# A two-layer diffusion block with expert-choice experts: the experts' residual in tiles of its own, later gathers, and weight rows loaded in pairs

## The chip, the cores and the metric

One core of one Trainium2 chip runs the whole program. The metric is the device time of the slowest (here the only) core in microseconds, as the median of several runs. TensorE does the matrix products, VectorE (DVE), ScalarE (ACT) and GpSimd (POOL) the elementwise work, and SyncE (SP) issues nearly all loads, in one queue, in the order of the program.

## The reference, cut to what matters

Two layers run over 256 latent tokens and 256 context tokens of width 1024 (the second layer finishes the latent tokens alone). Each layer is a token mixer with four branches, a layer norm, and an expert-choice feed-forward:

```python
def expert_choice_ffn(h, w_router, w_gate, w_up, w_down):
    aff = softmax(h @ w_router)                          # per token, over 16 experts
    gval, idx = top_k(swapaxes(aff, 1, 2), 32)           # each expert picks its 32 tokens
    xg = h[idx]                                          # gather
    y = (silu(xg @ w_gate) * (xg @ w_up)) @ w_down       # three 1024x1024 float32 matrices per expert
    y = y * gval[..., None]
    return zeros(n, 1024).at[idx].add(y)                 # scatter

x_lat = layer_norm(alpha * x_lat + g1 * y_lat, ln1_g, ln1_b)
f_lat = expert_choice_ffn(x_lat * (1 + sc2) + sh2, ...)
x_lat = layer_norm(alpha * x_lat + g2 * f_lat, ln2_g, ln2_b)
```

The context tokens go through the same code in the first layer with their own 32 picks per expert. All expert weights are read once in each layer: 16 experts x 3 matrices x 4 MiB = 192 MiB, so 384 MiB for both layers.

## The kernel before, in words

The change lies in `moe(l)` and in what feeds it. After `out_project` the normed tokens stand in `self.xz`, four tiles (layer 0) or two (layer 1) of 128 tokens x 1024. `route` transposes each with TensorE (eight 128x128 blocks) and multiplies them with the router's weights; then VectorE works out softmax and top-k, and `onehot` makes selection matrices from the positions.

**Gather.** `gather(g)` serves experts 4g to 4g+3. For each of the eight 128-wide blocks of the features, and for latent and context tokens apart, two matmuls with a block of `xz` as the stationary and the one-hot matrix as the moving operand bring the picked tokens, transposed, into `xgT`; ACT and DVE apply the layer norm's gain and shift (`c2`) on the way out of PSUM. The one-hot matmuls are in float32, and the trace counts two instructions for each. Gather 0 is interleaved with expert 0. Gathers 1 and 2 stand behind the gate and up matmuls of experts 1 and 2, and gather 3 behind the down matmuls of expert 2. There are four `xg` buffers.

**Residual.** Right behind gather 3, `residual()` broadcasts alpha times the norm's gain and shift over the partitions (32 matmul instructions, tile `ps_gb`) and overwrites `xz` with the residual term on VectorE. It must stand behind the last gather, since a gather reads the `xz` that it overwrites. After each fourth expert the experts' outputs are scattered into `xz` (`ps_f`), and after the last one into `ps_fin`, from which `ln_last` makes the layer's output.

**Weights.** `wl` loads one slot of 1 MiB: 256 rows of a weight matrix as two 128-row blocks, so each partition gets row p and row 128+p, 4 KB each. An expert needs twelve slots. The slots go round in the order of a list, `order2`: in layer 0 seven full slots (one tile of 8 KB per partition, one DMA) and six made of two 4 KB tiles (two DMAs); in layer 1 eleven full and seven split ones. A slot is loaded again when TensorE is done with its last content. Expert 0 has slots of its own besides (`early`), some in buffers of `xg`, so the loads of the first sixteen or so slots run before the experts begin. SP issues the loads in the program's order, so a load that waits for its slot holds up all behind it.

**The modulation weights.** `mod` loads 1 MiB pieces of `w_mod` with 8 KB runs through the same queue and the same tiles (line 234).

Of the kernel before, what the change touches and what calls it, by code (L numbers as in the profile page):

```python
# [15 lines left out]
P = 128  # L16
# [75 lines left out]
class Net:  # L92
# [1038 lines left out]
    def merge(self, l, br, first):  # L1131
# [3 lines left out]
        oT = self.mg.tile([P, 2, 512], F32, tag="oT", name="oTm", bufs=1)  # L1135
        nc.sync.dma_start(oT[:, :, :n], self.oT[br])
        ol = self.mg.tile([P, 2, 512], F32R, tag="ol", name="ol", bufs=1)
        oh = self.mg.tile([P, 2, 512], F32R, tag="oh", name="oh", bufs=1)
# [59 lines left out]

    def xt(self, t):

        return self.xz[:, t - self.xt0]
# [25 lines left out]
    def ln_last(self, l, t, src, rows):  # L1227

        nc = self.nc
        z = self.xt(t)  # L1230
# [13 lines left out]
    def comb(self, name, g, b, sc, sh):  # L1244

        nc = self.nc
        cg = self.keep.tile([P, 8], F32, name=name + "g")
        cb = self.keep.tile([P, 8], F32, name=name + "b")
# [3 lines left out]
        return cg, cb  # L1252


    def router_weights(self, l):
# [4 lines left out]
        nc.scalar.dma_start(wr, self.a["w_router"][l].rearrange("(k p) e -> p k e", p=P))  # L1260
# [15 lines left out]
    def route(self, t, stats):  # L1276
# [20 lines left out]
    def moe(self, l):  # L1297
# [10 lines left out]
        with ExitStack() as mo:  # L1308
# [11 lines left out]
            if nw == 2:  # L1320
                early = {x: [(px, "xg", 4)] for x in (7, 8, 9)}
                early[10] = [(mg, "ol", 1), (pe, "y1", 1)]
            else:
                early = {7: [(px, "xg", 4)] * 2, 8: [(px, "xg", 4), (mg, "ol", 1)]}

            def wl(src, e, kk):

                nonlocal cnt
                rows = src[l, e, kk * 256:(kk + 1) * 256, :].rearrange("(k p) f -> p k f", p=P)
# [5 lines left out]
                if not isinstance(slot, list):  # L1335
                    w = self.wload(rows, (2, 1024), pool=slot)
                    return [w[:, k] for k in range(2)]
                if len(slot) == 1:
                    pool, tag, n = slot[0]
                    w = pool.tile([P, 2, 1024], F32, tag=tag, name="we", bufs=n)  # L1340
                    nc.sync.dma_start(w, rows)
                    return [w[:, k] for k in range(2)]
# [55 lines left out]
            def gather(g):  # L1398

                xgT = px.tile([P, 8, 4, M], F32, tag="xg", name="xgT", bufs=4)  # L1400
# [6 lines left out]
                for kk in range(8 // kn):  # L1407
# [22 lines left out]
            def residual():  # L1430
# [3 lines left out]
                for j in range(2):  # L1434
# [14 lines left out]
            ys = rows = None  # L1449
            for e in range(NE):  # L1450
# [13 lines left out]
                if e in (1, 2):  # L1464
                    self.all_of(gather(e))
# [290 lines left out]
```

## Time and profile before

| | us |
|---|---|
| median of 3 runs | 2164.75 (2156.14 to 2170.97) |
| the profiled execution's own time | 2166.49 |
| its span | 2164.7 |
| layer 0: first gather to the end of the last expert's matmuls | 715.66 to about 1216 |
| layer 1: the same | 1692.15 to about 2155 |

The span is divided into stretches by what the DMA engines do. "DMA share" is the time that packets took on the core's 16 DMA engines, as a share of the stretch; it can go a little above 1, because packets overlap. A stretch at 1.02 or 1.03 is one in which the engines have no gap. MB in the rows is 10^6 bytes; a slot of 1 MiB is 1.049 MB. Busy time of PE is modelled at its ends, so full PE rows say only that work is queued without a gap.

### The profile page before, as it was taken

Reading aid. Unit: us, or ns where it says so; the run is one execution under the profiler, and the core shown is the slowest. Engines: PE = TensorE matmul, PEld = TensorE weight load, DVE = VectorE, ACT = ScalarE, POOL = GpSimd, SP = SyncE. Lnnn points to the kernel's source line nnn. Section 1 sums busy time; section 2 is a strip of 40 time slices with the busy share of each in tenths; the row PEclk is TensorE's granted clock in tenths of the full one; section 3 lists DMA queues with packets and bytes.
Section 4 is the critical chain, followed back from the end, with each engine's and each line's share of the span. In section 5 each row is a group of like instructions: output and inputs, shape, how many; then the busy total and the mean of one; then the engine's idle time right before and its main releaser. Section 6 shows DMA issues by size and latency. Waiting matters only on the chain. (4 is left out here: it accounts for less than half of the span.)

```text
span 2164.7 us, 33549 instructions
## 1 busy us (share of the span) xinstructions
PE 1849.5 (85%) x13730; PEld 1198.9 (55%) x13730; DVE 946.1 (44%) x2139; ACT 503.9 (23%) x1037; POOL 341.2 (16%) x366
## 2 busy tenths in 40 slices
PE   6899899988999899988887898898989886676665
PEld 2677778877879454322222576788889542222221
DVE  3859457854226324121121586967655330010102
ACT  2332217742221110000000332346443110000000
POOL 1151320014431000000000134321274000000000
PEclk9999999999999899999999998989999897776867
DMA  7546412137333599999999465303487899999996
GB/s 291 175 157 209 147 65 88 40 115 251 112 136 112 220 385 347 410 409 409 409 409 409 161 227 183 98 23 106 151 271 268 325 408 409 409 409 409 409 409 255
DMA packets 200182, 553.92 MB, mean 256 GB/s; under 512 B 16223, under 2 KB 83165, under 8 KB 194397
## 3 DMA queue, kind: packets, MB, share of 16 engines
q1 hardware_dynamic: 190960, 538.56, 66.2%
q10 hardware_dynamic: 9068, 13.23, 1.7%
q8 instruction: 108, 1.77, 0.3%
q14 instruction: 46, 0.37, 0.1%
HBM read 541.25 MB, written 10.49 MB: 255 GB/s over the span
## 5 line engine op out<-in xcount | busy, mean ns | idle before, releaser
L1461 PE MATMUL ps_gu<-w,xgT 128*32 128x256 f32 (+1 forms) x1632 | 241.5, 534 | 68.3 <-DMA w<-in_w_up_e_dram 35.0
L149 POOL TENSOR_TENSOR wl<-w,wh 128x1024 fp32r<-128x1024 f32 x62 | 155.2, 2503 | 894.6 <-ACT wh L148 805.4
L1461 PE MATMUL ps_gu<-we,xgT 128*32 128x256 f32 (+1 forms) x1440 | 204.0, 509 | 44.2 <-DMA we<-in_w_up_e_dram 26.3
L1461 PEld LDWEIGHTS ps_gu<-w,xgT 128*32 128x32 f32 (+1 forms) x1632 | 78.3, 134 | 210.5 <-issue 81.1
L1503 DVE TENSOR_TENSOR y<-ps_dn,g2r 32x512 f32<-32x512 f32 (+1 forms) x128 | 70.9, 554 | 254.3 <-PE ps_dn L1492 252.8
L311 PE MATMUL ps_gate<-hh,wh 128*128 128x512 f32 (+1 forms) x512 | 179.4, 351 | 0.4 <-ACT wh L148 0.4
L313 PE MATMUL ps_gate<-hh,wl 128*128 128x512 f32 (+1 forms) x512 | 179.7, 351 | 0.0
L312 PE MATMUL ps_gate<-hl,wh 128*128 128x512 f32 (+1 forms) x512 | 178.2, 348 | 0.0
L148 ACT CAST wh<-w 128x1024 fp32r<-128x1024 f32 x124 | 129.3, 1048 | 178.1 <-PE ps_gate L312 78.2
L1461 PEld LDWEIGHTS ps_gu<-we,xgT 128*32 128x32 f32 (+1 forms) x1440 | 62.0, 127 | 171.9 <-DMA we<-in_w_up_e_dram 63.7
L1492 PE MATMUL ps_dn<-w,eaT 128*32 128x256 f32 (+1 forms) x896 | 119.3, 524 | 28.8 <-DMA w<-in_w_down_e_dram 21.9
L1471 ACT ACTIVATE eth<-ps_gu 128x512 f32<-128x512 f32 (+1 forms) x32 | 15.7, 491 | 515.8 <-PE ps_gu L1461 515.8
L312 PE MATMUL ps_n<-wl,hh 128*128 128x256 f32 x400 | 116.6, 291 | 6.7 <-POOL wl L149 6.7
L1474 DVE SCALAR_TENSOR_TENSOR eac<-eth,ps_gu 128x512 f32<-128x512 f32 (+1 forms) x32 | 17.7, 555 | 238.9 <-PE ps_gu L1461 238.9
L311 PE MATMUL ps_n<-wh,hh 128*128 128x256 f32 x400 | 117.4, 294 | 5.5 <-DVE c_qk L872 3.6
L149 DVE TENSOR_TENSOR wl<-w,wh 128x1024 fp32r<-128x1024 f32 x62 | 85.8, 1384 | 72.4 <-ACT wh L148 72.1
L313 PE MATMUL ps_n<-wh,hl 128*128 128x256 f32 x400 | 116.7, 292 | 0.0
L1492 PE MATMUL ps_dn<-we,eaT 128*32 128x256 f32 (+1 forms) x640 | 91.2, 492 | 17.6 <-DMA we<-in_w_down_e_dram 13.2
L311 PEld LDWEIGHTS ps_gate<-hh,wh 128*128 128x128 f32 x512 | 98.9, 193 | 11.2 <-ACT wh L148 0.8
L313 PEld LDWEIGHTS ps_gate<-hh,wl 128*128 128x128 f32 x512 | 99.1, 193 | 10.8 <-DVE wl L149 0.2
L312 PEld LDWEIGHTS ps_gate<-hl,wh 128*128 128x128 f32 x512 | 98.7, 193 | 10.8
L1473 DVE SCALAR_TENSOR_TENSOR eth<-eth,ps_gu 128x512 f32<-128x512 f32 (+1 forms) x32 | 17.8, 555 | 193.6 <-ACT eth L1471 193.6
(452 smaller groups left out, 3579.4 us busy)
## 6 DMA issues: line engine op xcount, KB each, us to landing
w<-in_w_gate_e_dram SPq DMA_DIRECT2D x75, 1024.0 KB, 13.2
w<-in_w_down_e_dram SPq DMA_DIRECT2D x72, 1024.0 KB, 12.7
w<-in_w_up_e_dram SPq DMA_DIRECT2D x62, 1024.0 KB, 13.3
we<-in_w_up_e_dram SPq DMA_DIRECT2D x120, 512.0 KB, 13.6
w<-in_w_in_dram SPq DMA_DIRECT2D x54, 1024.0 KB, 5.6
we<-in_w_down_e_dram SPq DMA_DIRECT2D x108, 512.0 KB, 14.0
we<-in_w_gate_e_dram SPq DMA_DIRECT2D x96, 512.0 KB, 13.6
w<-in_w_mod_dram SPq DMA_DIRECT2D x44, 1024.0 KB, 5.1
```

Source lines behind the costliest of these rows:

```text
L148: nc.scalar.copy(h, w)
L149: (nc.gpsimd if j else nc.vector).tensor_tensor(x, w, h.bitcast(F32), op=OP.subtract)
L311: nc.tensor.matmul(ps, lh[k], rh[k], start=(k == 0), stop=False)
L312: nc.tensor.matmul(ps, lh[k], rl[k], start=False, stop=False)
L313: nc.tensor.matmul(ps, ll[k], rh[k], start=False, stop=(k == nk - 1))
L1461: nc.tensor.matmul(ps[M * q:M * q + M, :NF], xg[e // 4][:, 2 * kk + k, e % 4, :], w[k][:, q * NF:(q + 1) * NF], start=(kk == 0 and k == 0) ...
L1471: nc.scalar.activation(th, pss[0][:, :NF], AF.Tanh, scale=0.5)
L1473: nc.vector.scalar_tensor_tensor(th, th, 1.0, pss[0][:, :NF], op0=OP.add, op1=OP.mult)
L1474: nc.vector.scalar_tensor_tensor(ac, th, 0.5, pss[1][:, :NF], op0=OP.mult, op1=OP.mult)
L1492: nc.tensor.matmul(py[M * q:M * q + M, :NF], av[:, fc % nj, fc // nj, :], w[k][:, q * NF:(q + 1) * NF], start=(fc == 0), stop=(fc == 7))
L1503: nc.vector.tensor_tensor(ys[w][32 * e4:32 * e4 + 32, q * NF:(q + 1) * NF], py[o:o + 32, :NF], g2r[o:o + 32, q * NF:(q + 1) * NF], op=OP.mult)
```

## The change

1. The residual gets tiles of its own, `acc` (8 KB per partition for two token tiles: two of them in layer 0, one in layer 1). `residual()` reads `xz` and writes `acc`; the scatters, `fin_tiles` and, in layer 1, `ln_last` use `acc`. So `xz` stays whole, and the residual no longer needs all gathers ahead of it: it moves behind the down matmuls of expert 1.
2. Gathers 1, 2 and 3 move to behind the gate and up matmuls of experts 2, 6 and 10. Two `xg` buffers are left of four. The space is `acc`'s, and the early slots that lay in `xg` lie in `xg` and `acc`.
3. Layer 1's final norm rows are made at expert 11 in place of expert 9, in tiles of `xz`.
4. `wl` assigns rows in pairs: partition p gets rows 2p and 2p+1 of the 256, which lie side by side in HBM. A full slot is loaded as one run of 8 KB per partition; a split slot as two DMAs of 4 KB runs, each taking every other row.
5. So that the products still match, all that has the features on the partitions follows the pairs: the gather's stationary blocks, the router's transposes and the transposes of the activations take every other column (`pairs`, a step of two elements), the router's weights are loaded in that order, and `in_pairs` reorders the gains and shifts `c2` with small matmuls against every other column of the identity (16 in layer 0 and 8 in layer 1, each with a stationary block of 128x64 and four moving columns) and two VectorE copies.
6. Some small tiles share buffers across the layers (`comb`, `s2`), and `merge` takes its tile `oh` before `ol`.

```diff
+    def pairs(x):
+        return x.rearrange("p (a q j) -> p a j q", q=P, j=2)
...
+    def in_pairs(self, name, cols):
+        nc = self.nc
+        n = len(cols)
+        ps = self.pt.tile([P, 512], F32, tag="t", name="ps_pair")
+        pv = ps[:, :8 * n].rearrange("p (j i a) -> p j i a", j=2, i=n)
+        for i, c in enumerate(cols):
+            cv = c.rearrange("p (a h) -> p h a", h=2)
+            for h in range(2):
+                for j in range(2):
+                    nc.tensor.matmul(pv[64 * h:64 * h + 64, j, i], self.c("ident").rearrange("p (m j) -> p j m", j=2)[:, j],
+                                     cv[:, h], start=True, stop=True)
+        out = self.keep.tile([P, 4, 8], F32, tag="c2p", name=name, bufs=1)[:, :n]
+        for j in range(2):
+            nc.vector.tensor_copy(out.rearrange("p i (a j) -> p i a j", j=2)[:, :, :, j], pv[:, j])
+        return out
...
-        nc.scalar.dma_start(wr, self.a["w_router"][l].rearrange("(k p) e -> p k e", p=P))
+        nc.scalar.dma_start(wr.rearrange("p (a j) e -> p a j e", j=2),
+                            self.a["w_router"][l].rearrange("(a q j) e -> q a j e", q=P, j=2))
...
-                nc.tensor.transpose(ps[j][:, k * P:(k + 1) * P], z[:, kc * P:(kc + 1) * P], self.c("ident"))
+                nc.tensor.transpose(ps[j][:, k * P:(k + 1) * P], self.pairs(z)[:, kc // 2, kc % 2], self.c("ident"))
...
-                early = {x: [(px, "xg", 4)] for x in (7, 8, 9)}
+                early = {7: [(px, "xg", 2)], 8: [(px, "acc", 2)], 9: [(px, "acc", 2)]}
...
-                early = {7: [(px, "xg", 4)] * 2, 8: [(px, "xg", 4), (mg, "ol", 1)]}
+                early = {7: [(px, "acc", 1)], 8: [(px, "xg", 2), (mg, "ol", 1)]}
...
-                rows = src[l, e, kk * 256:(kk + 1) * 256, :].rearrange("(k p) f -> p k f", p=P)
+                rows = src[l, e, kk * 256:(kk + 1) * 256, :].rearrange("(p k) f -> p k f", k=2)
+                flat = src[l, e, kk * 256:(kk + 1) * 256, :].rearrange("(p k) f -> p (k f)", k=2)
...
-                    w = self.wload(rows, (2, 1024), pool=slot)
-                    return [w[:, k] for k in range(2)]
+                    w = self.wload(flat.unsqueeze(1), (1, 2048), pool=slot)
+                    return [w[:, 0, k * 1024:(k + 1) * 1024] for k in range(2)]
...
-                                nc.tensor.matmul(po, self.xz[:, off[w] + i, k * P:(k + 1) * P],
+                                nc.tensor.matmul(po, self.pairs(self.xz[:, off[w] + i])[:, k // 2, k % 2],
...
-                        z = self.xz[:, t, j * 512:(j + 1) * 512]
-                        nc.vector.tensor_tensor(z, z, gb[0], op=OP.mult)
+                        cs = slice(j * 512, (j + 1) * 512)
+                        z = acc[t // 2][:, t % 2, cs]
+                        nc.vector.tensor_tensor(z, self.xz[:, t, cs], gb[0], op=OP.mult)
                         nc.vector.tensor_tensor(z, z, gb[1], op=OP.add)
...
-                if e in (1, 2):
-                    self.all_of(gather(e))
-                if e == 9 and l == 1:
-                    rows = list(self.norm_rows(1, lambda nm: px.tile([P, 1024], F32, tag="xg", name=nm, bufs=4)))
+                if e in (2, 6, 10):
+                    self.all_of(gather(e // 4 + 1))
+                if e == 11 and l == 1:
+                    free = [self.xz[:, t] for t in range(2)]
+                    rows = list(self.norm_rows(1, lambda nm: free.pop(0)))
...
-                    nc.tensor.transpose(ps[:, j * P:(j + 1) * P], ac[:, j * P:(j + 1) * P], self.c("ident"))
+                    nc.tensor.transpose(ps[:, j * P:(j + 1) * P], self.pairs(ac)[:, j // 2, j % 2], self.c("ident"))
...
-                if e == 2:
-                    self.all_of(gather(3))
+                if e == 1:
+                    acc = [px.tile([P, 2, 1024], F32, tag="acc", name="acc", bufs=nw) for _ in ws]
                     residual()
...
-            self.c2 = {w: self.comb(f"c2_{l}{w}", ...) for w in ws}
+            cols = [self.comb(f"c2_{l}{w}", ...) for w in ws]
+            self.c2p = self.in_pairs(f"c2p{l}", [c[i] for i in range(2) for c in cols])
+            self.c2 = {w: (self.c2p[:, i], self.c2p[:, len(ws) + i]) for i, w in enumerate(ws)}
```

## Rows read from the trace of the kernel before

**Rows 1.** The page: mean busy share of the 16 DMA engines, forty slices, in tenths.

```profile
DMA  7546412137333599999999465303487899999996
```

**Rows 2.** Windows: us, busy us (instructions) of PE, PEld, DVE, ACT, POOL, PEclk, DMA share, GB/s.

```profile
754.00:860.00 106.00, 105.97 (x557) 55.64 (x553) 40.59 (x81) 14.96 (x31) 0.00 (x0) 1.00 0.91 356
860.00:1200.00 340.00, 290.20 (x1224) 87.36 (x1224) 62.69 (x104) 15.87 (x28) 0.00 (x0) 1.00 1.03 408
1700.00:2135.00 435.00, 309.14 (x3199) 125.48 (x3198) 60.28 (x140) 21.30 (x52) 0.00 (x0) 0.77 1.03 408
```

**Rows 3.** The same view, single windows of 10 us.

```profile
750.00:760.00 10.00, 10.00 (x50) 5.73 (x48) 2.74 (x4) 0.00 (x0) 0.00 (x0) 1.00 0.41 143
...
820.00:830.00 10.00, 10.00 (x80) 8.59 (x81) 7.55 (x15) 2.08 (x5) 0.00 (x0) 1.00 0.47 192
...
1690.00:1700.00 10.00, 9.36 (x71) 7.06 (x72) 3.58 (x14) 1.96 (x4) 0.00 (x0) 0.78 0.22 70
1700.00:1710.00 10.00, 10.00 (x145) 6.01 (x148) 1.65 (x5) 1.70 (x4) 0.00 (x0) 1.00 1.01 368
```

**Rows 4.** SP's waits in 754 to 832 us: us in total, times, longest.

```profile
SPq L127 <- PE ps_dn L1492: 32.7, 4, 12.5
SPq L1346 <- PE ps_gu L1461: 17.3, 14, 11.8
```

**Rows 5.** TensorE's timeline: start, us, instructions; where experts 1, 2, gather 3, expert 3 begin.

```profile
754.20 3.17 PE L1461 MATMUL ps_gu<-w,xgT 128*64 128x512 f32 x13
...
785.62 4.40 PE L1461 MATMUL ps_gu<-w,xgT 128*64 128x512 f32 x18
...
816.91 2.87 PE L1416 MATMUL ps_xg<-OH,xz 128*128 128x128 f32 x22
...
828.08 1.94 PE L1461 MATMUL ps_gu<-we,xgT 128*64 128x512 f32 x8
```

**Rows 6.** Windows with the gathers' tile ps_xg alone: PE, PEld, DVE, ACT, PEclk, DMA, GB/s.

```profile
768.00:785.70 17.70, 8.93 (x64) 7.77 (x64) 3.19 (x8) 3.65 (x8) 1.00 0.86 337
```

**Rows 7.** Windows with the residual's tile ps_gb alone: PE, PEld, DVE, PEclk, DMA, GB/s.

```profile
819.00:828.30 9.30, 4.23 (x32) 3.89 (x32) 3.08 (x6) 1.00 0.62 249
```

**Rows 8.** DMA packets of 900 to 1100 us, when expert weights alone are loaded.

```profile
DMA packets 21782, 81.85 MB, mean 409 GB/s; under 512 B 1822, under 2 KB 1822, under 8 KB 21774
```

**Rows 9.** SP's timeline from 1308 us, then DMA packets of 1315:1318, 1316:1318 and 227:230.

```profile
1313.07 0.80 SPq L127 DMA_DIRECT2D w<-in_w_mod_dram  x2
...
DMA packets 171, 1.27 MB, mean 423 GB/s; under 512 B 16, under 2 KB 16, under 8 KB 16
...
DMA packets 124, 0.88 MB, mean 442 GB/s; under 512 B 16, under 2 KB 16, under 8 KB 16
...
DMA packets 166, 1.25 MB, mean 415 GB/s; under 512 B 15, under 2 KB 15, under 8 KB 15
```

**Rows 10.** The page's DMA issues: count, KB each, median us to landing; the full slots.

```profile
w<-in_w_gate_e_dram SPq DMA_DIRECT2D x75, 1024.0 KB, 13.2
w<-in_w_down_e_dram SPq DMA_DIRECT2D x72, 1024.0 KB, 12.7
w<-in_w_up_e_dram SPq DMA_DIRECT2D x62, 1024.0 KB, 13.3
```

**Rows 11.** Weight loads of TensorE, ns min/median/max: the route's, the gathers', and a broadcast column's.

```profile
L1287 PEld LDWEIGHTS ps_xT<-const,xz x48: 137/141/228, 686.2 to 1678.1; 128*128 128x128 f32 x48
...
L1416 PEld LDWEIGHTS ps_xg<-OH,xz x384: 186/192/338, 715.7 to 1746.6; 128*128 128x128 f32 x192
...
L1440 PEld LDWEIGHTS ps_gb<-const,lgb x64: 185/190/192, 819.5 to 1751.7; 128*128 128x128 f32 x64
```

**Rows 12.** The chain that ended last, ahead of layer 1's output projection: start, us, what.

```profile
1648.18 1.78 PE ps_rb L164 x16
1649.96 1.92 PE ps_wrb L1268 x16
```

More of the change, by code (lines that the diff above doesn't have):

```diff
@@ L1225, in ln_hat, with ln_last @@
         nc.vector.tensor_scalar(z, z, mu, rs, op0=OP.subtract, op1=OP.mult)
-    def ln_last(self, l, t, src, rows):
+    def ln_last(self, l, t, src, rows, z):
         nc = self.nc
-        z = self.xt(t)
         mu, rs = self.ln_stats(t, src)
@@ L1246, in comb @@
         nc = self.nc
-        cg = self.keep.tile([P, 8], F32, name=name + "g")
-        cb = self.keep.tile([P, 8], F32, name=name + "b")
+        c = self.keep.tile([P, 2, 8], F32, tag=name[:2] + name[-1], name=name, bufs=1)
+        cg, cb = c[:, 0], c[:, 1]
         nc.vector.tensor_tensor(cg, g, sc, op=OP.mult)
@@ L1335, in wl @@
                 if not isinstance(slot, list):
-                    w = self.wload(rows, (2, 1024), pool=slot)
-                    return [w[:, k] for k in range(2)]
+                    w = self.wload(flat.unsqueeze(1), (1, 2048), pool=slot)
+                    return [w[:, 0, k * 1024:(k + 1) * 1024] for k in range(2)]
                 if len(slot) == 1:
                     pool, tag, n = slot[0]
-                    w = pool.tile([P, 2, 1024], F32, tag=tag, name="we", bufs=n)
-                    nc.sync.dma_start(w, rows)
-                    return [w[:, k] for k in range(2)]
+                    w = pool.tile([P, 2048], F32, tag=tag, name="we", bufs=n)
+                    nc.sync.dma_start(w, flat)
+                    return [w[:, k * 1024:(k + 1) * 1024] for k in range(2)]
                 out = []
@@ L1448, in moe @@
             g0 = next(first)
-            ys = rows = None
+            ys = rows = acc = None
             for e in range(NE):
@@ L1482, in moe @@
                 if e == NE - 1:
-                    fin = {off[0] + i: self.fin_tiles(off[0] + i, pool, tag) for i, (pool, tag) in
+                    fin = {off[0] + i: self.fin_tiles(acc[off[0] // 2][:, i], pool, tag) for i, (pool, tag) in
                            enumerate(((self.pg, "g"), (self.pm, "m")))}
@@ L1521, in moe @@
                     if e == NE - 1 and nw == 2:
-                        fin.update({off[1] + i: self.fin_tiles(off[1] + i, pool, tag) for i, (pool, tag) in
+                        fin.update({off[1] + i: self.fin_tiles(acc[off[1] // 2][:, i], pool, tag) for i, (pool, tag) in
                                     enumerate(((self.pt, "t"), (self.pa, "s")))})
@@ L1531, in moe @@
                                     if hf:
-                                        self.ln_last(l, t + self.xt0, fin[t], rows)
+                                        self.ln_last(l, t + self.xt0, fin[t], rows, self.xz[:, t] if l == 0 else acc[0][:, t])
                                     continue
@@ L1543, in fin_tiles @@
             r.append(pool.tile([P, 512], F32, tag=tag, name="ps_fin"))
-            self.nc.tensor.matmul(r[hf], self.c("ident"), self.xz[:, i, hf * 512:hf * 512 + 512], start=True, stop=False)
+            self.nc.tensor.matmul(r[hf], self.c("ident"), z[:, hf * 512:hf * 512 + 512], start=True, stop=False)
         return r
@@ L1661, in run @@
             v = self.vec[l]
-            s2_ = self.keep.tile([P, 8, 2], F32, name=f"s2{l}")
+            s2_ = self.keep.tile([P, 8, 2], F32, tag="s2", name=f"s2{l}", bufs=1)
             nc.vector.tensor_scalar_add(s2_, self.modc[l][:, 32:40, :], 1.0)
             ws = [0, 1] if l == 0 else [0]
-            self.c2 = {w: self.comb(f"c2_{l}{w}", v[:, R_L1G:R_L1G + 8], v[:, R_L1B:R_L1B + 8], s2_[:, :, w], self.mcol(l, 3, w)) for w in ws}
+            cols = [self.comb(f"c2_{l}{w}", v[:, R_L1G:R_L1G + 8], v[:, R_L1B:R_L1B + 8], s2_[:, :, w], self.mcol(l, 3, w)) for w in ws]
+            self.c2p = self.in_pairs(f"c2p{l}", [c[i] for i in range(2) for c in cols])
+            self.c2 = {w: (self.c2p[:, i], self.c2p[:, len(ws) + i]) for i, w in enumerate(ws)}
             self.g1r = {}
```

9 lines of the change are left out of this document (5 added, 4 removed).

## The prediction

> **What bounds the kernel now.** Read the page's line of DMA shares first [rows 1]: two plateaus of nines, one for each layer's experts. Then the windows [rows 2]: from 860 to 1200 us and from 1700 to 2135 us the DMA share is 1.03 at 408 GB/s, that is, the 16 engines move expert weights without a gap. TensorE is full for 85% of the time in the first plateau (290.2 of 340 us, granted clock 1.00) and for 71% in the second (309.1 of 435 us, granted clock 0.77). In the plateaus the time is bytes over rate, and no engine's work counts. So two things can shorten the experts: a plateau that begins earlier, or a higher rate.
>
> Ahead of layer 0's plateau, 754 to 860 us, it is the other way round: TensorE is busy for 105.97 of 106 us and the DMA moves 356 GB/s in place of 408 [rows 2], with holes of 143 and 192 GB/s [rows 3]. SP's waits say why: it stands up to 12.5 us at a time for slots that `ps_dn` or `ps_gu` still holds [rows 4]. TensorE can't free them, since it does gathers. Layer 1 has no such stretch: its only hole is 1690:1700 us (share 0.22), when expert 0 has just begun, and from 1700 us on the share is 1.01 [rows 3], with gathers 1 to 3 still to come. There TensorE's work is hidden already.
>
> **Gathers and residual: layer 0's plateau begins earlier.** Expert 1 with gather 1 takes 785.62 - 754.20 = 31.4 us of TensorE, expert 2 with gather 2 816.91 - 785.62 = 31.3, gather 3 with the residual 828.08 - 816.91 = 11.2 [rows 5]. One gather is 8.9 us [rows 6], so an expert alone is about 22.4 us, and the residual's matmuls are 4.2 us [rows 7]. The DMA needs 12 x 1.049 MB / 408 GB/s = 30.8 us for an expert. TensorE alone outruns the DMA by 8 us per expert; with a gather in each expert it doesn't.
>
> Now the order after. Expert 0 ends at 754 us as before. Expert 1 without a gather ends at 776.5, the residual at 781, expert 2 with gather 1 at 812, expert 3 at 835 (before: expert 3 began at 828 and so ended about 851). On the DMA side, loads for expert 2 begin as before at 754.5 us, flow from about 756, and are done at 787. Loads for expert 3 need the slots of experts 1's end and expert 2, one after the other: thirteen slots go round, so the first needs expert 1's last slot (776.5), and the k-th later one needs expert 2's k-th, free at 781 + 1.87k. The DMA gets to them at 787 + 2.57k, so it is always later than the slot, also behind the gather (the ninth slot is free at 781 + 8.9 + 16.8 = 806.7, and wanted at 810). The DMA doesn't starve again. All bytes of 754 to 860 us, 106 x 356 = 37.7 MB, then take 37.7 MB / 408 GB/s = 92.5 us from 756, to 848.5: **11.5 us** saved. The most is the whole hole, 106 x (1 - 356/408) = 13.5; if half of the starvation stays, it is 6.
>
> Gathers 2 and 3 fall in the plateau. A pause of 8.9 us there delays the freeing of slots by as much. A slot loaded is used at once and not wanted again for 13 loads, 33 us, so the pause fits; and TensorE wins it back in two experts at 8 us each, with four experts between the gathers. Price 0; without that cover it would be up to 2 x 8.9 = 17.8 us in layer 0. In layer 1 the gathers are half as large (one token group), with eighteen slots. Moved instructions on the other queues: the gathers' 16 evacuations each on DVE and ACT, the residual's on DVE. Neither engine bounds the stretch (DVE 40.6 of 106 us, ACT 15.0 [rows 2]). On DVE the residual now stands ahead of expert 1's `y`, as it stood ahead of expert 2's. No DMA moves past another on SP. Layer 1's norm rows at expert 11 sit in slack: 0. Layer 1's residual and gathers save nothing, as its DMA is full from 1700 us.
>
> **8 KB runs: the rate.** In the plateau nearly all packets are under 8 KB (21774 of 21782) and the rate is 409 GB/s [rows 8]. The trace of before has the other kind too: two `w_mod` loads of 1 MiB in 8 KB runs are issued at 1313.07 us, and while they flow only the small completion writes are under 8 KB (16 of 171 packets) at 423 GB/s [rows 9]; the inner 2 us show 442, another such burst at 227 us 415 [rows 9]. A slot then takes 1.0486 MB / 423 = 2.479 us against 2.564, **0.085 us less**. I take 423, the widest window without the burst's ragged end; the ends are 415 (0.037 us) and 442 (0.192 us), and below them no gain.
>
> How many slots: the full ones alone, 209 named `w` [rows 10] of 384 slots, and by the rotation some 222 with those named `we`; it has 7 full of 13 in layer 0 and 11 of 18 in layer 1. Only those count that the DMA loads while it is the bound. Layer 0: experts 2 to 15, 168 slots x 7/13 = 90. Layer 1: 435 us x 408 GB/s = 177 MB, 169 slots x 11/18 = 103. Together 193 x 0.085 = **16.4 us** (7 at 415, 37 at 442, 0 if packet size doesn't matter). Split slots read every other 4 KB row and keep 4 KB packets; I take no change, since the `w_mod` rows lie 24 KB apart and flow at full rate.
>
> [...] The trace's 423 against 409 is 3.4%, from a window of only 3 us.
>
> **What is added.** `in_pairs` puts 24 small matmuls, 48 instructions, ahead of the output projection of the two layers. This stretch is on TensorE's path: the chain shows 16 `ps_rb` instructions for 1.78 us and 16 `ps_wrb` for 1.92 us right there [rows 12]. At 0.115 us each the cost is 48 x 0.115 = 5.5 us if all is on the path and 0 if it slips into a gap; I take **4 us**, as the neighbours are on the path. The two VectorE copies and the router's load in pairs are small beside it.
>
> Stationary blocks with a step of two columns are new. No row shows one. The nearest are the contiguous blocks (141 and 192 ns) and the broadcast column, step zero, 190 ns [rows 11]: the step made no difference there, so I take 0. The other end is twice the time (third rival); a gain is excluded, as nothing is read less.
>
> **The sum.** 11.5 + 16.4 - 4 = 23.9 us off the profiled execution's 2166.5 gives 2142.6; the median is 1.7 us below that execution, so **2141 us**, -1.1%. Its own range, from the ends of the terms, is 2130 to 2150.
>
> **Rivals.**
> *Packet size is worth little.* Speaks for it: the bursts last 2 to 3 us, and one is at 415. Then the 8 KB runs give 0 (the plateau's 409) to 7 us (the burst at 415): 2150 to 2157. Against it: both bursts are above 409, though they hold their own ragged start. Chance 0.2. [...]
>
> *The starvation only moves.* If the expert without gather is slower than 22.4 us, or the scheduler lets gather 1 run ahead of the down matmuls of expert 2 long enough to hold the slots, layer 0's hole stays by half or more, and a late gather opens a new one: the 11.5 us shrink to 0 to 4, 2149 to 2153. For it: the slack found above is only 3 us at the ninth slot. Chance 0.15.
>
> *Strided weight loads are slow.* If a stationary block of every other column took twice its time, the route pays 48 x 0.141 = 6.8 us, all ahead of the top-k; gather 0 pays 64 x 0.192 = 12.3 us in layer 0 and 6.1 in layer 1, where TensorE holds the first slots; and gather 1 in layer 0 another 12.3, of which 3 hide: 34 us in all, so 2175, slower than before by 10. It decides from 1.7 times the contiguous load: there it cancels the 24 us. Against it: a step of zero costs nothing [rows 11]. [...] Chance 0.06.
>
> **How the numbers follow.** The sum as forecast 0.57 (with 0.02 left for a rate at the upper end, down to 2120), the rivals 0.2, 0.15, 0.06. About 1%, 21 us, is what a measurement of this kernel can tell from no change, so the line is at 2143. The forecast lies just beyond it: of its 0.57 I count 0.46 as faster by over 1%, with the upper end 0.48, and a little for a rival beside a higher rate, 0.5. Same: the rest of it, the first two rivals and half of the third, 0.46. Slower by over 1% needs strided loads well over twice as slow: 0.04. The range 2124 to 2158 leaves out the third rival and the ends of the rate.
>
> **What would show it.** In layer 0 after: no SP wait over 5 us between 756 us and the end of expert 3, and DMA windows at 1.02 or more from 756 us on. In both plateaus: 415 to 420 GB/s in place of 409, the page's packets fewer by some 28,000 (222 full slots x 128). Weight loads of `ps_xg` still near 192 ns. `ps_pair` with 48 instructions, some 5 us of PE. Layer 1's stretch from its first gather to the end shorter by 8 to 9 us and layer 0's by 19. The forecast is wrong if the plateau's rate stays at 409, if 754 to 860 us still has windows under 300 GB/s, or if a hole opens behind experts 6 or 10.

## The result, and the profile after

The changed kernel takes 2150.36 us (median of 10 runs, 2136.43 to 2162.71) against 2169.03 us for the kernel before (10 runs, 2156.14 to 2174.48): a ratio of 0.9911, 95% interval 0.9888 to 0.9934. By the ratio that is 19.3 us less; the medians themselves are 18.7 us apart. The forecast was 2141 us with a range of 2124 to 2158. The profiled execution took 2152.02 us (span 2150.2).

First the windows over the same three stretches as in [rows 2]: us, busy us (instructions) of PE, PEld, DVE, ACT and POOL, granted clock, DMA share, GB/s. Then single windows of 10 us, as in [rows 3].

```profile
757.00:848.00 91.00, 89.90 (x427) 41.20 (x425) 36.06 (x67) 7.69 (x15) 0.00 (x0) 1.00 1.00 404
848.00:1188.00 340.00, 311.01 (x1367) 108.67 (x1364) 68.06 (x119) 23.29 (x45) 0.00 (x0) 1.00 1.02 414
1693.00:2120.00 427.00, 302.23 (x3196) 129.72 (x3192) 60.22 (x140) 21.28 (x52) 0.00 (x0) 0.80 1.02 415
```

```profile
750.00:760.00 10.00, 10.00 (x48) 5.66 (x48) 2.39 (x4) 0.21 (x1) 0.00 (x0) 1.00 0.47 172
760.00:770.00 10.00, 10.00 (x49) 5.51 (x46) 1.04 (x2) 0.60 (x1) 0.00 (x0) 1.00 1.01 389
...
820.00:830.00 10.00, 9.22 (x42) 3.62 (x39) 1.38 (x2) 0.60 (x1) 0.00 (x0) 1.00 1.03 417
```

The hole of layer 0 is gone: where 820 to 830 us had 192 GB/s, it has 417, and the plateau now begins some 3 us after expert 0's end. TensorE is nearly as full as before in 757 to 848 us (89.90 of 91 us); it only does other things first. SP's waits in 758 to 848 us have shrunk with it, from 12.5 us at the longest [rows 4] to 6.2. (The wait that ends with expert 0, ahead of this window, is as long as before, 11.1 and 11.0 us.)

```profile
SPq L127 <- PE ps_dn L1518: 11.4, 4, 6.2
SPq L127 <- PE ps_gu L1485: 8.0, 8, 1.3
```

Second, the rate. The DMA packets of 900 to 1100 us, for [rows 8]:

```profile
DMA packets 16746, 83.09 MB, mean 415 GB/s; under 512 B 1860, under 2 KB 1860, under 8 KB 11361
```

415 GB/s in place of 409, with nearly half of the packets under 8 KB gone (the whole execution has 170597 packets, 29,585 fewer than before's 200182). Third, the price. The weight loads and matmuls that the pairing touches, ns min/median/max, for [rows 11]:

```profile
L1309 PEld LDWEIGHTS ps_xT<-const,xz x48: 197/209/264, 688.4 to 1670.4; 128*128 128x128 f32 x48
...
L1439 PEld LDWEIGHTS ps_xg<-OH,xz x384: 192/196/336, 718.1 to 1968.7; 128*128 128x128 f32 x192
...
L1504 PEld LDWEIGHTS ps_aT<-const,eac x96: 194/209/222, 748.8 to 2122.5; 128*128 128x128 f32 x96
...
L1268 PE MATMUL ps_pair<-c,const x48: 201/201/226, 488.8 to 1638.2; 128*64 128x4 f32 x48
```

A block of every other column costs a gather's load 4 ns, but a transpose's 68 ns (141 before, 209 after). And the chain ahead of layer 1's output projection, for [rows 12] (start, us, what):

```profile
1637.84 0.62 PE ps_pair L1268 x16
1638.49 0.24 DVE c2p L1272 x2
1638.73 0.33 DVE thm L1163
1639.05 3.08 DVE ml L1175 x3
1642.13 0.41 DVE wrs L1287 x2
1642.55 0.14 issue
1642.69 1.94 PE ps_wrb L1290 x16
```

`ps_wrb` used to follow `ps_rb` at once. Now its operand `wrs` needs the reordered gains, and on VectorE's queue `wrs` comes to stand behind three of `ml`'s splits.

Where the time went, by stretches of the profiled executions. The marks are first and last instructions in TensorE's timeline: the first `ps_gu` of a layer, the last `ps_dn` of an expert, the last `ps_br` of layer 1. "Middle" is all from layer 0's last `ps_dn` to layer 1's last `ps_br`, which is the layer's end, modulation, token mixing; the clock beside it is the granted one of that stretch. (us)

| kernel | start to first ps_gu | expert 0 | experts 1 to 15, layer 0 | middle, clock | to first ps_gu, layer 1 | expert 0 | experts 1 to 15, layer 1 |
|---|---|---|---|---|---|---|---|
| before | 720.2 | 34.2 | 452.5 | 441.2, 0.93 | 46.4 | 17.9 | 434.5 |
| after | 722.9 | 34.6 | 434.6 | 445.8, 0.93 | 49.2 | 18.1 | 426.8 |
| after_again | 726.6 | 34.6 | 435.0 | 441.3, 0.95 | 53.5 | 18.1 | 426.7 |
| gathers_only | 717.5 | 34.2 | 430.0 | 440.2, 0.93 | 46.4 | 17.9 | 423.2 |
| gathers_128 | 719.6 | 34.2 | 441.2 | 435.1, 0.96 | 46.2 | 17.9 | 434.8 |
| runs_only | 724.9 | 34.6 | 448.6 | 445.6, 0.93 | 49.0 | 18.2 | 426.5 |
| no_late_gathers | 724.2 | 34.6 | 434.5 | 445.6, 0.93 | 49.2 | 18.1 | 427.7 |
| before_aligned | 724.2 | 34.2 | 443.4 | 436.6, 0.95 | 46.2 | 18.1 | 423.1 |
| before_64 | 724.7 | 34.2 | 452.6 | 445.7, 0.92 | 46.8 | 17.9 | 433.8 |
| router_plain | 724.6 | 34.6 | 434.7 | 449.2, 0.92 | 47.4 | 18.7 | 427.3 |
| step8 | 721.1 | 39.1 | 447.0 | 444.5, 0.93 | 49.6 | 21.0 | 424.8 |
| after_aligned | 731.3 | 34.6 | 428.0 | 437.6, 0.95 | 53.3 | 18.1 | 420.0 |
| all_full | 724.5 | 34.6 | 430.6 | 430.0, 0.95 | 47.5 | 19.0 | 421.7 |
| best | 728.2 | 34.6 | 427.5 | 425.4, 0.96 | 47.6 | 18.1 | 417.4 |

From before to after the experts give 17.9 + 7.7 = 25.6 us; the other columns take about 11 back. The middle's share of that (4.6 us) can't be put down to the change: after and after_again are the same kernel and differ there by 4.5 us, the longer one at the lower granted clock. The expert columns of these two repeat within 0.4 us. So the parts are read from those, and the whole from the medians.

### The profile page after: what moved, and what is told of

Same layout as the page of the kernel before. It is cut to its first block, busy times and chain, and to the rows that moved or that the text cites. A ratio compares the mean times of both kernels' runs of the same rounds, so it can differ in the third digit from the quotient of the medians.

```text
span 2150.2 us, 33641 instructions
## 1 busy us (share of the span) xinstructions
PE 1854.2 (86%) x13778; PEld 1218.0 (57%) x13778; DVE 950.5 (44%) x2143; ACT 503.0 (23%) x1037; POOL 338.3 (16%) x366
## 2 busy tenths in 40 slices
DMA packets 170597, 553.92 MB, mean 258 GB/s; under 512 B 15182, under 2 KB 82124, under 8 KB 136268
## 5 line engine op out<-in xcount | busy, mean ns | idle before, releaser
L1485 PE MATMUL ps_gu<-we,xgT 128*32 128x256 f32 (+1 forms) x1440 | 197.8, 492 | 35.5 <-DMA we<-in_w_up_e_dram 20.2
L1518 PE MATMUL ps_dn<-we,eaT 128*32 128x256 f32 (+1 forms) x640 | 92.0, 498 | 14.3 <-DMA we<-in_w_down_e_dram 10.4
## 6 DMA issues: line engine op xcount, KB each, us to landing
w<-in_w_up_e_dram SPq DMA_DIRECT2D x62, 1024.0 KB, 13.5
we<-in_w_gate_e_dram SPq DMA_DIRECT2D x96, 512.0 KB, 13.4
```

The costliest lines, as they stand in the source:

```text
L1485: nc.tensor.matmul(ps[M * q:M * q + M, :NF], xg[e // 4][:, 2 * kk + k, e % 4, :], w[k][:, q * NF:(q + 1) * NF], start=(kk == 0 and k == 0) ...
L1518: nc.tensor.matmul(py[M * q:M * q + M, :NF], av[:, fc % nj, fc // nj, :], w[k][:, q * NF:(q + 1) * NF], start=(fc == 0), stop=(fc == 7))
```

## The experiments

**gathers_only: the new order of gathers, residual and buffers, with rows, slots and router as before.**

```diff
-        return x.rearrange("p (a q j) -> p a j q", q=P, j=2)
+        return x.rearrange("p (a j q) -> p a j q", q=P, j=2)
...
-                rows = src[...].rearrange("(p k) f -> p k f", k=2)
+                rows = src[...].rearrange("(k p) f -> p k f", p=P)
...
-            self.c2p = self.in_pairs(...)
```

> The changed kernel with its old order of weight rows: residual in its own tiles, gathers 1 to 3 at experts 2, 6 and 10, but 4 KB runs, no strided blocks, no reordering matmuls. My theory (the hole of layer 0 is worth 11 us by itself, and nothing is paid for it): 10 to 13 us faster than before, a ratio of 0.994 to 0.995, layer 0 from the end of expert 0 to its last down matmul 11 us shorter, layer 1's experts unchanged, plateaus at 408 to 409 GB/s. Rival (all of the gain is the higher rate, the starvation only moves): within 3 us of before.

2132.84 us against 2167.17, ratio 0.9832 (0.9783 to 0.9882): half of the change is at least as fast as the whole. Its packets in 900 to 1100 us say where that comes from:

```profile
DMA packets 22330, 83.96 MB, mean 420 GB/s; under 512 B 1857, under 2 KB 1857, under 8 KB 22321
```

All packets are still of 4 KB, and yet the rate is 420 GB/s, above the 415 of the changed kernel. Neither theory has this. What differs beside the order is only where tiles lie: this kernel has no tile `c2p` and fewer small tiles than before, so that in the built program the first slot of weights begins at byte 35584 of a partition and nearly all others lie whole multiples of 4096 bytes further on; in before, after and runs_only the first is at 35712. 35584 is a multiple of 256; 35712 is 128 beyond one. The runs before_aligned, gathers_128 and before_64 test that.

**runs_only: the pairs and the 8 KB runs, with the old order of gathers and residual.**

```diff
-                if e in (2, 6, 10):
-                    self.all_of(gather(e // 4 + 1))
+                if e in (1, 2):
+                    self.all_of(gather(e))
...
-                if e == 1:
-                    acc = [px.tile([P, 2, 1024], F32, tag="acc", name="acc", bufs=nw) for _ in ws]
+                if e == 2:
+                    self.all_of(gather(3))
                     residual()
```

> The changed kernel with its old schedule: gathers 1 and 2 at experts 1 and 2, gather 3 and the residual behind expert 2 in place, but the weight rows in pairs with 8 KB runs, strided blocks and reordering matmuls. My theory (rate worth 14 us, the additions cost some 6): 6 to 10 us faster than before, plateaus at 414 to 416 GB/s, the hole of layer 0 between 820 and 830 us back at under 250 GB/s. Rival (packet size is worth little and the gathers bring it all): 0 to 6 us slower than before, as only the additions are left.

2167.17 us, ratio 0.9983 (0.9949 to 1.0017). In 900 to 1100 us it has 416 GB/s, and layer 1's experts take 426.5 us as in the changed kernel. In layer 0 the hole is back, at 830 to 840 us:

```profile
760.00:770.00 10.00, 10.00 (x49) 5.62 (x47) 3.04 (x5) 0.60 (x1) 0.00 (x0) 1.00 0.92 343
820.00:830.00 10.00, 10.00 (x72) 8.06 (x68) 4.94 (x10) 3.21 (x8) 0.00 (x0) 1.00 0.99 369
830.00:840.00 10.00, 10.00 (x64) 5.84 (x64) 9.71 (x17) 0.46 (x1) 0.00 (x0) 1.00 0.37 111
```

The faster loads only wait longer for TensorE there, so layer 0 gains 3.9 us alone, and 6.6 with the new order (441.2 to 434.6, gathers_128 to after). The columns ahead of the experts are 2.6 and 4.7 us longer and take more than half of the 11.9 us of both layers back. What is left isn't to be told from no gain (3.7 us by the ratio, -3.7 to 11.1): neither the expected 6 to 10 us faster nor the rival's loss is shown.

**after_again: the changed kernel once more, as a yardstick.**

> The changed kernel once more, unchanged, beside the others. It says how much of the difference between two profiled executions lies in stretches that the change doesn't touch. In the first trace the stretch between layer 0's last expert and layer 1's output projection is some 4 us longer than before, outside the reordering matmuls. If that is chance, it comes out between -5 and 5 us here; if the change causes it, it is 4 us again. The ratio: 0.989 to 0.993.

2145.84 us, ratio 0.9879 (0.9825 to 0.9934): the result repeats. Its middle is 441.3 us, 0.1 longer than before, so the 4 us more of the first trace do not repeat. (Its 53.5 us ahead of layer 1's experts are taken up further down.)

**no_late_gathers: gathers 2 and 3 left out; experts 8 to 15 use the tokens of gather 1.**

```diff
-                                nc.tensor.matmul(..., xg[e // 4][:, 2 * kk + k, e % 4, :], ...)
+                                nc.tensor.matmul(..., xg[min(e // 4, 1)][:, 2 * kk + k, e % 4, :], ...)
...
-                if e in (2, 6, 10):
-                    self.all_of(gather(e // 4 + 1))
+                if e == 2:
+                    self.all_of(gather(1))
```

> The changed kernel without gathers 2 and 3: experts 8 to 15 work on the tokens gathered for experts 4 to 7, so the output isn't the reference's, with all weights loaded and all matmuls done. My theory (a late gather in the plateau is hidden, as the slots hold 33 us of loads): within 3 us of the changed kernel. Rival (a late gather holds up the loads for its 9 us in layer 0 and 5 us in layer 1, at two places each): 15 to 28 us faster than the changed kernel.

2149.22 us, ratio 0.9907 (0.9873 to 0.9941): the same time without the work. The plateaus don't change either, while PE's busy time falls from 311.01 to 293.42 us:

```profile
848.00:1188.00 340.00, 293.42 (x1238) 89.80 (x1238) 62.40 (x103) 15.86 (x28) 0.00 (x0) 1.00 1.02 414
1693.00:2120.00 427.00, 300.91 (x3144) 121.70 (x3136) 56.15 (x128) 17.65 (x44) 0.00 (x0) 0.78 1.02 415
```

Late gathers are hidden: the rival's 15 to 28 us are excluded. But they are not the pauses of 8.9 us that the prediction priced. In layer 0 of the changed kernel TensorE ran gather 2 in two halves, at 853 to 867 and 907 to 921 us, and gather 3 at 971 to 980 and 1021 to 1034 us, in pieces of 2 to 16 instructions among the `ps_gu` matmuls, the longest of 2.5 us:

```profile
906.74 0.74 PE L1439 MATMUL ps_xg<-OH,xz 128*128 128x128 f32 x4
...
971.02 2.50 PE L1439 MATMUL ps_xg<-OH,xz 128*128 128x128 f32 x16
```

What one pause of 8.9 us in the plateau would cost, no run tests.

**before_aligned, gathers_128, before_64: where the slots begin.** before_aligned is the kernel before with its small tiles shared, as the change does it, and nothing else; the slots then begin at a multiple of 256. gathers_128 is gathers_only with an unused tile of 128 bytes in front, before_64 is before_aligned with one of 64 bytes.

```diff
-        cg = self.keep.tile([P, 8], F32, name=name + "g")
-        cb = self.keep.tile([P, 8], F32, name=name + "b")
+        c = self.keep.tile([P, 2, 8], F32, tag=name[:2] + name[-1], name=name, bufs=1)
+        cg, cb = c[:, 0], c[:, 1]
...
-            s2_ = self.keep.tile([P, 8, 2], F32, name=f"s2{l}")
+            s2_ = self.keep.tile([P, 8, 2], F32, tag="s2", name=f"s2{l}", bufs=1)
```

```diff
+        pad = self.cpool.tile([P, 32], F32, name="pad")
+        nc.vector.memset(pad, 0.0)
```

> The kernel before, with only the small tiles of comb and s2 shared as in the changed kernel. That takes 128 bytes per partition out of the pool that lies ahead of the weight slots, so the slots start at a multiple of 256 bytes in SBUF (35584 in place of 35712 and so on), as they do in gathers_only and neither before nor after. New theory (the slots' start sets the rate: packets of 4 KB at a constant 159 ns and 420 GB/s when they start at a multiple of 256, 159 to 172 ns and 409 GB/s at 128 beyond one): plateaus at 419 to 420 GB/s, the hole of layer 0 as before, 20 to 25 us faster than before, ratio 0.988 to 0.991. Rival (gathers_only was fast by where its inputs lay in HBM, or by chance): 409 GB/s and within 4 us of before.

> gathers_only with an unused tile of 128 bytes ahead of the slots, so that they start at 35712 and so on, as before. New theory: plateaus back at 409 GB/s, 9 to 13 us faster than before instead of 34, which is the gathers' part alone. Rival (the schedule itself gives the 34 us): 30 us or more faster than before, 420 GB/s.

> The kernel before with its small tiles shared, as in before_aligned, and an unused tile of 64 bytes, so that the slots of weights begin 64 beyond a multiple of 256. If a start at a multiple of 64 is all that a transfer needs, the kernel before (128 beyond) would not have been slower, so this is not the rule; if it is 256, the plateau is 409 GB/s or less and the time is that of before (ratio 0.995 to 1.0); if what counted in before_aligned was that the small tiles are shared and not the start, it keeps 420 and 0.990.

Packets of 900 to 1100 us; before_aligned first:

```profile
DMA packets 22358, 83.97 MB, mean 420 GB/s; under 512 B 1879, under 2 KB 1879, under 8 KB 22350
```

gathers_128:

```profile
DMA packets 21789, 81.85 MB, mean 409 GB/s; under 512 B 1827, under 2 KB 1827, under 8 KB 21781
```

before_64:

```profile
DMA packets 21774, 81.82 MB, mean 409 GB/s; under 512 B 1819, under 2 KB 1819, under 8 KB 21766
```

before_aligned: 2146.09 us, ratio 0.9905 (0.9874 to 0.9936), so moving all slots by 128 bytes is worth as much as the whole change (2165.23 - 2146.09 = 19.1 us). gathers_128: 2159.63, 0.9974 (0.9952 to 0.9997). before_64: 2169.74, 1.0013 (0.9995 to 1.0031). The rate follows the start of the slots: 420 GB/s at a multiple of 256 bytes, 409 at 64 or 128 beyond. The packets say the same: of the 4 KB packets in 900 to 1100 us, nearly all take 159 ns in gathers_only and before_aligned, and 159 to 172 ns, 163 in the mean, in before, gathers_128 and before_64. gathers_128 also gives the price of the new order by itself: layer 0's experts take 441.2 us in place of 452.5, layer 1's 434.8 in place of 434.5. gathers_only against before_aligned is a second such pair, both at the better start: 430.0 in place of 443.4, and 423.2 in place of 423.1.

**after_aligned and all_full: the same start for the changed kernel, and whole slots.** after_aligned writes the reordered gains over the others, so that no tile is added. all_full leaves the start as it is and merges the pairs of 4 KB tiles, so that nearly every slot is one 8 KB run.

```diff
-        out = self.keep.tile([P, 4, 8], F32, tag="c2p", name=name, bufs=1)[:, :n]
+        out = self.c2t[:, :n]
```

```diff
-        return [self.whs[self.nwh].tile([P, 1024], F32R, tag=g, name=g)[:, :n] for g in ("wh", "wl")]
+        t = self.whs[self.nwh].tile([P, 2048], F32R, tag="whl", name="whl")
+        return [t[:, :n], t[:, 1024:1024 + n]]
...
-            order2 = order + [self.wp] * self.NW + [[(self.whp, "wh", 3), (self.whp, "wl", 3)]] * 3
+            order2 = order + [self.wp] * self.NW + [[(self.whp, "whl", 3)]] * 3
```

> The changed kernel with the reordered gains written over their source tile, which takes 128 bytes out and puts the slots at a multiple of 256. New theory (start and packet size both count): 8 KB packets at a constant 309 ns, plateaus at 424 to 430 GB/s, 10 to 20 us faster than the changed kernel, ratio to before 0.979 to 0.985. Rival (the start alone counts, and 8 KB runs only make up for a bad start): plateaus at 420, as in gathers_only, and 3 to 8 us slower than gathers_only by the strided transposes and the reordering.

> The changed kernel with the hi and lo tiles of the split weights and the bh and bl tiles allocated as one tile each, so that 12 of 13 slots in layer 0 and 17 of 18 in layer 1 are full and load in 8 KB runs; the slots start 128 beyond a multiple of 256 as in the changed kernel. Theory (a cost per packet, whatever the start): plateaus at 418 to 420 GB/s in place of 415, 5 to 10 us faster than the changed kernel. Rival (the mix has nothing more to give): 415, the same time.

after_aligned: 2136.37 us, ratio 0.9854 (0.9824 to 0.9884), 423 GB/s in 900 to 1100 us, both just short of what the first theory expected, the rate above the rival's 420. But at the better start the pairs give little: against gathers_only the experts' columns are 2.0 and 3.2 us shorter, and the whole is not shown to be faster (ratio to before 0.9854 against 0.9832). all_full: 2129.86, 0.9832 (0.9805 to 0.9859), with these packets:

```profile
DMA packets 12395, 84.07 MB, mean 420 GB/s; under 512 B 1372, under 2 KB 1372, under 8 KB 2908
```

So 8 KB runs are worth 409 to 420 when nearly all slots have them and none begins at a multiple of 256; the changed kernel has a little over half of that. By the ratios all_full is some 10 to 17 us faster than the changed kernel, where 5 to 10 were expected; the experts' columns hold 9.1 us of it. Its middle, which uses the merged tiles too, is with 430.0 us shorter than any but best's; why, no run tells.

**best: whole slots, aligned, with the router in the old order and the gains reordered behind the output projection.** Beside the edits of all_full and, for the start of the slots, of after_aligned:

```diff
-        for w, (cg, cb) in self.c2.items():
+        for w, (cg, cb) in self.c2r.items():
...
-                nc.tensor.transpose(ps[j][...], self.pairs(z)[:, kc // 2, kc % 2], self.c("ident"))
+                nc.tensor.transpose(ps[j][...], z[:, kc * P:(kc + 1) * P], self.c("ident"))
...
+            self.c2r = {w: cols[i] for i, w in enumerate(ws)}
...
+            c2p = self.in_pairs(f"c2p{l}", [c[i] for i in range(2) for c in cols])
+            self.c2 = {w: (c2p[:, i], c2p[:, len(ws) + i]) for i, w in enumerate(ws)}
             self.moe(l)
```

> All slots whole 8 KB, slots at a multiple of 256 bytes, the router's transposes and weights in the old order of rows, and the gains' reordering issued behind L1's attention output instead of ahead of its router. If the size of the runs and the start of the slots are two separate causes, they add: a plateau near 427 GB/s against 420 for either nearly alone and 409 for neither; from all_full's 2130 us some 860 us of loads at 420 instead of 427 are 14 us less, and the router's part some 4 less: about 2112 us, ratio 0.972 to 0.979, faster than every kernel so far. If they are one cause (a limit of 420 to 423 reached either way), the plateau stays at 423 and the time at 2126 to 2132.

2119.45 us (4 runs, 2116.47 to 2122.49) against 2165.48, ratio 0.9791 (0.9773 to 0.9809): the shortest median of all. The ratio lies at the edge of what the two causes together let expect, the rate nearly at the expected 427. (Against all_full the experts' columns are 3.1 and 4.3 us shorter, where 14 us were expected; the middle is 4.6 us shorter once more.)

```profile
DMA packets 12567, 85.27 MB, mean 426 GB/s; under 512 B 1397, under 2 KB 1397, under 8 KB 2933
```

409, 420, 420 and 426 GB/s for neither, start alone, size alone and both: they are two causes, and they add for the most part.

**router_plain: the changed kernel with only the router back in the old order** (the same edit as in best; the gains are still reordered in the old place).

> The changed kernel with the router's transposes and weights in the old order, the experts' gathers still reordered. If the strided weight loads and the wait for the reordered gains are the cost seen around the routers, ps_xT's weight loads go back from 209 to 141 ns, PE no longer waits for wrs between ps_rb and ps_wrb, L1's out_project goes from 49 to 53 us to 46 to 47, and the time is 3 to 6 us below the changed kernel's (ratio 0.984 to 0.988). If these parts lie beside other work, the time equals the changed kernel's (0.988 to 0.991). The plateau stays at 415 to 416 GB/s in both.

The mechanism is nearly as expected. The transposes' loads, and TensorE's timeline ahead of layer 1's output projection:

```profile
L1308 PEld LDWEIGHTS ps_xT<-const,xz x48: 138/141/228, 689.5 to 1673.4; 128*128 128x128 f32 x48
```

```profile
1643.04 0.67 PE L1268 MATMUL ps_pair<-c,const 128*64 128x4 f32 x16
1643.64 2.05 PE L164 MATMUL ps_rb<-const,modc 128*128 128x128 f32 x16
1645.64 1.87 PE L1289 MATMUL ps_wrb<-wrs,ones 128*128 128x32 f32 x16
```

No wait is left, and the stretch to layer 1's first `ps_gu` is 47.4 us against 49.2 and 53.5 (46 to 47 were expected). But the time isn't shorter: 2149.41 us, ratio 0.9930 (0.9908 to 0.9952), where the changed kernel has 0.9911 and 0.9879. A gain of more than some 3 us is excluded by that (0.9911 - 0.9930 = -0.0019, with both intervals' half-widths of 0.0023 combined 0.0032). The expectation of 3 to 6 us fell. The profiled execution of router_plain had the longest middle of all, at a granted clock of 0.92:

```profile
1194.00:1643.00 449.00, 402.26 (x3478) 353.88 (x3478) 315.69 (x693) 184.07 (x371) 154.10 (x175) 0.92 0.45 149
```

Whether that is chance or goes with the edit, these runs don't tell.

**step8: a step of eight columns** in the router's transposes and the gathers (so it computes another function than the reference).

```diff
-        return x.rearrange("p (a q j) -> p a j q", q=P, j=2)
+        a = x.shape[-1] // 256
+        return x.rearrange("p (q a j) -> p a j q", a=a, j=2)
```

> The changed kernel with a stationary step of 8 columns instead of 2 in the router's transposes and the gathers, and of 4 and 2 in the transposes of the experts' activations; the permutation is then not the one of the weights' rows, so it computes another function. If a step beyond one column costs a weight load a fixed part, ps_xT's loads stay at 209 ns and the gathers' at 196, and the time at the changed kernel's. If the cost grows with the step, because fewer columns come from one read, ps_xT goes well beyond 250 ns, the gathers too, and out_project of L1 is 5 us or more longer.

Half of each theory holds:

```profile
L1310 PEld LDWEIGHTS ps_xT<-const,xz x48: 186/193/255, 685.2 to 1684.7; 128*128 128x128 f32 x48
...
L1440 PEld LDWEIGHTS ps_xg<-OH,xz x384: 312/334/338, 714.7 to 1987.2; 128*128 128x128 f32 x192
```

The transposes don't mind eight columns more than two (193 and 209 ns), but the gathers' loads go from 196 to 334 ns. Why the one grows with the step and the other doesn't, no run shows. The time is 2166.1 us, ratio 1.0000 (0.9973 to 1.0028): the change's gain is gone. Expert 0 takes 39.1 and 21.0 us in place of 34.6 and 18.1, and layer 0's other experts 447.0 in place of 434.6. The longer gathers hold the slots, and the DMA starves again, 373 GB/s in place of the changed kernel's 413 for the same window. Gather 1 takes TensorE 18.4 us (799.1 to 817.5) in place of 11.4 (796.4 to 807.7), and towards its end the rate falls:

```profile
760.00:848.00 88.00, 86.93 (x402) 45.35 (x398) 28.46 (x56) 7.70 (x15) 0.00 (x0) 1.00 0.94 373
...
810.00:820.00 10.00, 10.00 (x39) 6.31 (x40) 2.03 (x7) 1.86 (x4) 0.00 (x0) 1.00 0.59 242
```

## Why the prediction was right, and where it was not

**What bounds the kernel: right.** no_late_gathers takes 17.6 us of TensorE's work out of layer 0's plateau and the time stays; 128 bytes of address, which change no engine's work, take 19 us off.

**Gathers and residual, -11.5 us: right.** Layer 0's experts are 452.5 - 441.2 = 11.3 us shorter with the order alone (gathers_128), layer 1's unchanged, as said; the pair at the better start gives 443.4 - 430.0 = 13.4 us. SP still waited once for 6.2 us, above the 5 named as the mark, but behind loads that were still running: the DMA share stayed at 1.01 and more in each 10 us from 760 us on. No hole opened behind experts 6 or 10 either. The timed runs of gathers_128 show less than the column, 5.6 us (0.6 to 10.4), which leaves the 11.5 out; its profiled execution was the shortest of the twelve, with a short middle. The other two pairs of kernels that differ by the order alone (before_aligned and gathers_only, runs_only and after) lie some 16 us apart by their ratios. So the 11 us are shown in the experts' stretch, and in the whole the sign, with a size between 6 and 16.

**Gathers 2 and 3 at 0: right in the price**, by no_late_gathers, but not for the reason given: in layer 0 there was no pause of 8.9 us for the slots to cover, since TensorE took the late gathers in pieces of at most 2.5 us.

**8 KB runs, -16.4 us: nearly right in the sum, wrong in its two factors.** Layer 1 gained 434.5 - 426.8 = 7.7 us (8.8 forecast: 103 slots), layer 0 6.6 behind the order (7.7 forecast: 90 slots), together 14.3. But a full slot is loaded at 420 GB/s (all_full), not 423: 1.0486 MB / 420 = 2.497 us, 0.067 us less in place of 0.085. The 423 of the `w_mod` burst [rows 9] came from 3 us of trace. 14.3 us / 0.067 us would be 213 slots, more than the 193 counted as bound by the DMA. That one factor was too large and the other too small is luck. The split slots' 4 KB packets took 163 ns in the mean before and after, so their 0 stood.

**Start of the slots and size of the runs.** With slots at a multiple of 256 bytes, 8 KB runs gave 426 GB/s (best) against 420 for 4 KB runs (gathers_only, before_aligned), 1.4% more. At the start that this kernel's slots have, 128 beyond, it is 420 (all_full) against 409 (before), 2.7%. The packets of 900 to 1100 us agree: those of 4 KB took 163 ns in the mean in before and in after, those of 8 KB 314 in after, some 12 less than two of 4 KB. Why the start counts, no run shows. The rival "packet size is worth little" was thus wrong here, where a 4 KB packet takes 163 ns and not 159. With aligned slots it would have been right: the pairs then take 2.0 + 3.2 = 5.2 us off the experts (gathers_only to after_aligned), in place of 14.3.

**in_pairs, +4 us: too much for the instructions, and what hangs on them was left out.** The 48 instructions take TensorE 0.67 us in layer 1 and 1.17 in layer 0, 1.8 us in all (the mark said some 5): 0.04 us each, not the 0.115 of the neighbours. What the prediction had not is VectorE's queue, behind which `ps_wrb` waits 1.1 us. The price shows in the stretch from layer 1's last `ps_br` to its first `ps_gu`. It takes 46.2 to 46.8 us in the five kernels with the old order of rows; 47.4 to 47.6 in router_plain, all_full and best, which have pairs but no wait of `ps_wrb`; 49.0 to 49.6 in four of the six executions with the wait; and 53.5 and 53.3 in the other two, after_again and after_aligned. In these two the granted clock was 0.50 for 6.8 us right behind the wait, as in after_again (the wait stands in brackets; granted clock 0.50, then DMA share and GB/s):

```profile
1642.30 2.95 PE L1290 MATMUL ps_wrb<-wrs,ones 128*128 128x32 f32 x16 [1.09 <-DVE wrs L1287]
...
1643.00:1649.80 6.80, 6.80 (x34) 6.80 (x34) 1.39 (x6) 0.00 (x0) 0.00 (x0) 0.50 0.67 276
```

In none of the eight executions without the wait did it fall there. Whether the wait brings the fall on is not shown. The 68 ns on each transpose are hardly paid: all_full has them within its 47.5 us, and from layer 0's first transpose to its first `ps_gu` it is 34.4 us after the change and 33.9 before. The stretch ahead of layer 0's experts is too spread to tell more: before_aligned, which has none of these edits, needs 724.2 us where before needs 720.2. And router_plain, which takes the wait away, is not faster as a whole, so how much of all this the whole pays is open. The argument that failed is "the step made no difference there" for a step of zero: at two columns it made next to none for the gathers, 48% for the transposes.

**The sum.** -11.3 - 14.3 = -25.6 us in the experts against -27.9 forecast; the whole is 19.3 shorter by the ratio (14.3 to 24.3), which leaves 6.3 us (1.3 to 11.3) for all that was added in place of 4. The likeliest case came out, with a gain 4.6 us smaller than forecast: 2.3 of them the two gains, 2.3 the costs. Most of the rest between 2141 and 2150 us lies in the kernel before, whose median is 2169.03 here and was 2164.75 when the forecast was made. At 0.9% the result falls just short of the line of 1% that the prediction drew: it is the case called same (chance 0.46), not faster (0.5). The ends of the terms as listed (6 to 13.5, 7 to 37, 5.5 to 0) add up to 2114 to 2157 us, so "its own range" of 2130 to 2150 is narrower than they are. Of the other marks 29,585 packets fewer (28,000), `ps_pair` with 48 instructions and layer 0's experts shorter by 17.9 us (19) stood; 5 us of `ps_pair` did not.

**Rivals.** "The starvation only moves" is refuted by the windows. "Strided weight loads are slow" named the right place with a threshold of 1.7 times: the transposes reached 1.48 (209 / 141 ns), the gathers 1.02 (196 / 192); step8, where the gathers reach 1.74 (334 / 192), gives back the whole gain, as that rival said it would.

## What to carry to other kernels

Where a plateau of loads is the bound, look at where the destination tiles begin as well as at the size of the runs: 128 bytes of small tiles in front of the slots were worth as much here as the whole change, and an edit that adds a small tile can take that away unseen. Check such a change again when the destination moves: the 8 KB runs took 14.3 us off the experts at the worse start and 5.2 at the better one. Move TensorE's optional work into a stretch where the DMA is the bound, and see in the trace in what pieces it runs there: a gather of 11.4 us left no hole, one of 18.4 us did. And when a part of an edit does as well as the whole, compare rates in the same window before looking for a mechanism in the schedule.

## What the runs showed of the hardware that was not expected

In these runs the rate of the weight loads from HBM into SBUF went with the start of the destination: 409 GB/s for 4 KB runs at 64 or 128 bytes beyond a multiple of 256, 420 at a multiple; with nearly all runs of 8 KB 420 (128 beyond) and 426 (at a multiple). Other starts were not tried. A weight load of a transpose with a step of two or eight columns took 209 or 193 ns against 141, while a gather's load, with the same tile as its stationary, took 192, 196 and 334 ns for steps of one, two and eight. Behind a wait of TensorE of 1.1 us the granted clock was 0.50 for 6.8 us in two of six executions, and the stretch around it took 4 us longer in those two.
